# Gate and up projections by seven half-width products in place of eight, with the weight sums on GpSimd

## The chip, the core and the metric

The kernel runs on one core of a Trainium2 chip. TensorE (PE) multiplies, VectorE (DVE), ScalarE (ACT) and GpSimd (POOL) do the elementwise work, SyncE (SP) issues most of the DMAs. The metric is the device time of one execution in microseconds. Before the change the median of three runs is 1285.59 us (1284.54 to 1286.78).

## The reference

Two layers of a decoder over 512 positions of width 1024. The part that the change touches is the feed-forward block of each layer:

```
h = rmsnorm(x, g_pre_ffn[l])
f = silu(h @ w_gate[l]) * (h @ w_up[l])      # (512, 1024) @ (1024, 2816)
f = f @ w_down[l]                            # (512, 2816) @ (2816, 1024)
x = x + rmsnorm(f, g_post_ffn[l])
```

Ahead of it stands a mixing sub-layer: one input projection, four attention groups of four heads, and an output projection with a norm and a residual addition. All values are float32.

## The kernel before

Every float32 operand of a matmul is kept as a pair of reduced-precision tiles, hi and lo: `hi` is a cast (ScalarE) and `lo` the difference of the value and hi (VectorE or GpSimd). A product is three matmuls, `mm3` (lines 195 to 198): hi by hi, hi by lo, lo by hi, all into one PSUM bank. Activations stay transposed on chip, 128 rows of the width by 512 positions per tile, so a block of 128 columns of a weight matrix is the stationary operand and the positions are the moving one.

`weights` (line 160) loads 128x512 values, casts them (line 168) and makes the differences (line 171 on GpSimd, 173 on VectorE; `pool_share` says which chunk goes to GpSimd, and 0 means none). Five raw buffers (WRAW) and six pairs of split buffers (WSPL) go round.

In `ffn` a weight matrix has KF = 22 blocks of 128 columns. For every block j the gate product takes 8 steps over the width, 24 matmuls of 512 columns into one bank, and the up product the same. Then ScalarE applies Silu to the gate bank (line 836) and VectorE multiplies it by the up bank (line 837) into `f`. The down projection follows, with all eight banks as accumulators.

The stage begins while the mixing sub-layer ends. The four row blocks of 128 positions are closed one after the other (`close`, line 738: residual addition, two norms, lines 744 to 749), transposed on TensorE (line 222) and split into `h` (`norm_turn`, line 230). To bridge the wait for the last two of them, the first two blocks of gate and up are computed in halves of 256 positions: first the left halves of all four, then the right halves. The transposes of row blocks 2 and 3 (`turns`) are issued after the second and the fourth left half.

The program is written in one thread; a scheduler puts each engine's instructions in an order and sets the waits between engines. Each engine then works through its own list in that order, so an instruction that waits holds up all behind it on its engine. Tiles with the same tag share a fixed number of buffers, and a new tile waits for the last reader of the old one.

Of the kernel before, what the change touches and what calls it, by code (L numbers as in the profile page):

```python
# [9 lines left out]
F32 = mybir.dt.float32  # L10
# [6 lines left out]
P = 128  # L17
# [59 lines left out]
def f32(ap):  # L77
    return ap.bitcast(F32)
# [3 lines left out]
def decoder(ctx, tc, x, positions, w_in, b_forget, g_mla_q, w_mla_q_up, g_mla_kv, w_mla_kv_up,  # L82
# [190 lines left out]
    def mixing(l, h_in, in_slots, out_slots, w_first):  # L273
# [464 lines left out]
        def close(t, ys):  # L738
# [12 lines left out]
            def turn(behind):  # L751
                with tc.issue_after(behind.ins):
                    norm_turn(t, norm_transpose(hn), h2)
# [3 lines left out]
        turns = []  # L757
# [39 lines left out]
        return xt, h2, turns[2:]  # L797

    def ffn(l, xt, h, turns, f_slots, after):
        fq = []  # L800
# [4 lines left out]
        def w_of(src, j, into=(None, None)):  # L805
            cs = slice(j * P, (j + 1) * P)
            return [weights(src[l, 4 * i * P:4 * (i + 1) * P, cs].rearrange("(k p) c -> p k c", p=P), [4, P], into=into[i])
                    for i in range(2)]

        def block(ps, w, hs):  # L810
            for k in range(KD):
                hi, lo = w[k // 4]
                mm3(ps[:, hs], hi[:, k % 4, :], lo[:, k % 4, :], h[0][k // 4][:, k % 4, hs], h[1][k // 4][:, k % 4, hs],
                    k == 0, k == KD - 1)

        pool_share[0] = SHARE_FFN
        room = keep.tile([P, 6, 512], F32R, name="w_half", tag="slotE")
        room = [room[:, i, :].rearrange("p (k c) -> p k c", c=P) for i in range(4)]
        halves = [(bank(ps_mm, "ps_g"), w_of(w_gate, 0)), (bank(ps_mm, "ps_u"), w_of(w_up, 0)),
                  (bank(ps_mm, "ps_g"), w_of(w_gate, 1)), (bank(ps_o, "ps_u"), w_of(w_up, 1, (room[0:2], room[2:4])))]  # L820
        for hs in (slice(0, 256), slice(256, 512)):
            for i, (ps, w) in enumerate(halves):
                block(ps, w, hs)
                if i % 2 == 1 and turns:
                    turns.pop(0)(last_mm[0])
# [114 lines left out]
```

## Time and profile before

| | |
|---|---|
| runs | 1284.54, 1285.59, 1286.78 us |
| profiled execution | 1284.56 us, span 1282.6 us |
| mean granted TensorE clock | 0.998 |
| busy: PE, DVE, ACT, POOL | 97%, 51%, 46%, 16% |
| gate/up stage, first layer | 279.69 to 524.51 us |
| gate/up stage, second layer | 912.16 to 1156.46 us |

A start time of a row counts from the start of the span. The records of neighbouring instructions of one engine overlap a little, so two in a row take less than the sum of their records; the step from start to start is the time that counts for a stream. "128x512" is partitions by elements. A row with x2 stands for two instructions in a row, with their time together. Where a row names an idle time in brackets, the releaser behind it is what ended it.

### The profile page before, as it was taken

Reading aid. Unit: us, or ns where it says so; the run is one execution under the profiler, and the core shown is the slowest. Engines: PE = TensorE matmul, PEld = TensorE weight load, DVE = VectorE, ACT = ScalarE, POOL = GpSimd, SP = SyncE. Lnnn points to the kernel's source line nnn. Section 1 sums busy time; section 2 is a strip of 40 time slices with the busy share of each in tenths; the row PEclk is TensorE's granted clock in tenths of the full one; section 3 lists DMA queues with packets and bytes.
Section 4 is the critical chain, followed back from the end, with each engine's and each line's share of the span. In section 5 each row is a group of like instructions: output and inputs, shape, how many; then the busy total and the mean of one; then the engine's idle time right before and its main releaser. Section 6 shows DMA issues by size and latency. Waiting matters only on the chain.

```text
span 1282.6 us, 17740 instructions
## 1 busy us (share of the span) xinstructions
PE 1242.6 (97%) x6314; PEld 1041.9 (81%) x6314; DVE 657.0 (51%) x1307; ACT 591.0 (46%) x1287; POOL 201.2 (16%) x287
## 2 busy tenths in 40 slices
PE   6999999999999999999999999999999999999998
PEld 6878877789888888888787788778888888888886
DVE  5876866774333233333466668677742233333334
ACT  6676756754222223333456767666532222233332
POOL 3213334430000000000131324433300000000001
PEclk9999999999999999999999999999999999999999
DMA  7321242522333333333342222334233333332332
GB/s 231 83 59 42 63 117 55 170 75 84 98 99 99 96 94 98 97 94 97 123 125 71 59 56 69 99 91 132 83 107 97 95 96 99 99 98 89 95 97 75
DMA packets 158329, 122.01 MB, mean 95 GB/s; under 512 B 9120, under 2 KB 133152, under 8 KB 158240
## 3 DMA queue, kind: packets, MB, share of 16 engines
q1 hardware_dynamic: 152192, 112.07, 29.8%
q10 hardware_dynamic: 6048, 8.80, 2.6%
q8 instruction: 50, 0.82, 0.3%
q14 instruction: 39, 0.32, 0.1%
HBM read 112.45 MB, written 4.19 MB: 91 GB/s over the span
## 4 chain that ended last, share of the span: by engine, by line
PE 73%; DVE 3%; ACT 3%; DMA 2%; issue 2%; POOL 2%; ACTq 0%; DVEq 0%; POOLq 0%; SPq 0%
PE ps_g L197 6%; PE ps_g L196 6%; PE ps_u L197 6%; PE ps_u L198 6%; PE ps_u L196 6%; PE ps_g L198 6%; PE ps_d L196 6%; PE ps_d L198 6%; PE ps_d L197 6%; PE ps_s L453 2%; PE ps_out L198 2%; PE ps_out L197 2%; PE ps_out L196 2%; PE pT L473 2%; PE ps_qk L196 1%
## 5 line engine op out<-in xcount | busy, mean ns | idle before, releaser
L168 ACT CAST whi<-wraw 128x512 fp32r<-128x512 f32 x348 | 214.2, 621 | 478.4 <-PE ps_g L197 167.4
L173 DVE TENSOR_TENSOR wlo<-wraw,whi 128x512 fp32r<-128x512 f32 (+1 forms) x329 | 239.0, 731 | 368.1 <-ACT whi L168 367.7
L197 PE MATMUL ps_g<-h,whi 128*128 128x512 f32 (+1 forms) x384 | 144.0, 375 | 2.9 <-DVE h L230 2.9
L196 PE MATMUL ps_g<-h,whi 128*128 128x512 f32 (+1 forms) x384 | 143.9, 375 | 1.0 <-ACT h L230 0.8
L198 PE MATMUL ps_g<-h,wlo 128*128 128x512 f32 (+1 forms) x384 | 143.4, 373 | 0.0
L198 PE MATMUL ps_u<-h,wlo 128*128 128x512 f32 (+1 forms) x352 | 133.7, 380 | 0.0
L196 PE MATMUL ps_u<-h,whi 128*128 128x512 f32 (+1 forms) x352 | 133.7, 380 | 0.0
L197 PE MATMUL ps_u<-h,whi 128*128 128x512 f32 (+1 forms) x352 | 133.7, 380 | 0.0
L239 POOL TENSOR_SCALAR rstd<-ssp 128x1 f32<-128x1 f32 x16 | 7.0, 438 | 708.2 <-ACT jk L235 708.1
L198 PE MATMUL ps_d<-whi,fl 128*128 128x512 f32 x288 | 112.2, 389 | 0.0
L196 PE MATMUL ps_d<-whi,fh 128*128 128x512 f32 x288 | 112.1, 389 | 0.0
L197 PE MATMUL ps_d<-wlo,fh 128*128 128x512 f32 x288 | 112.1, 389 | 0.0
L464 POOL TENSOR_SCALAR pr<-pr,den 128x128 f32<-128x128 f32 (+3 forms) x128 | 77.8, 624 | 192.7 <-DVE den L461 189.2
L197 PEld LDWEIGHTS ps_g<-h,whi 128*128 128x128 f32 x384 | 73.0, 190 | 16.5 <-DVE h L230 4.2
L196 PEld LDWEIGHTS ps_g<-h,whi 128*128 128x128 f32 x384 | 73.0, 190 | 14.8 <-ACT h L230 2.3
L198 PEld LDWEIGHTS ps_g<-h,wlo 128*128 128x128 f32 x384 | 73.0, 190 | 12.4
L196 PE MATMUL ps_qk<-h,whi 128*128 128x512 f32 x192 | 76.8, 400 | 0.0
L196 PEld LDWEIGHTS ps_u<-h,whi 128*128 128x128 f32 x352 | 66.2, 188 | 12.5
L198 PEld LDWEIGHTS ps_u<-h,wlo 128*128 128x128 f32 x352 | 66.3, 188 | 12.4
L197 PEld LDWEIGHTS ps_u<-h,whi 128*128 128x128 f32 x352 | 66.2, 188 | 12.4
L198 PE MATMUL ps_qk<-h,wlo 128*128 128x512 f32 x192 | 75.8, 395 | 0.0
L197 PE MATMUL ps_qk<-h,whi 128*128 128x512 f32 x192 | 75.8, 395 | 0.0
(272 smaller groups left out, 2557.7 us busy)
## 6 DMA issues: line engine op xcount, KB each, us to landing
wraw<-in_w_gate_dram SPq DMA_DIRECT2D x88, 256.0 KB, 2.9
wraw<-in_w_up_dram SPq DMA_DIRECT2D x88, 256.0 KB, 2.9
wraw<-in_w_down_dram SPq DMA_DIRECT2D x88, 256.0 KB, 2.8
wraw<-in_w_in_dram SPq DMA_DIRECT2D x72, 256.0 KB, 3.1
wraw<-in_w_out_dram SPq DMA_DIRECT2D x32, 256.0 KB, 3.0
xt<-in_x_dram SPq DMA_DIRECT2D x16, 256.0 KB, 4.6
rope_b<-rope_a ACTq DMA_DIRECT2D x64, 64.0 KB, 2.0
wraw<-in_w_in_dram SPq DMA_DIRECT2D x16, 178.0 KB, 3.4
```

Of the source, the lines that this page charges most:

```text
L168: nc.scalar.copy(hi, raw)
L173: nc.vector.tensor_tensor(lo, raw, f32(hi), op=ALU.subtract)
L196: nc.tensor.matmul(ps, a_hi, b_hi, start=start, stop=False)
L197: nc.tensor.matmul(ps, a_hi, b_lo, start=False, stop=False)
L198: last_mm[0] = nc.tensor.matmul(ps, a_lo, b_hi, start=False, stop=stop)
L239: nc.gpsimd.tensor_scalar(r, ss[:, 0:1], ss[:, 1:2], EPS, op0=ALU.add, op1=ALU.add)
L453: nc.tensor.matmul(ps[:, 0:w], a if a.shape[-1] == P else a[:, qt * P:(qt + 1) * P], b[:, 0:w], start=i == 0, stop=i == n - 1)
L464: nc.gpsimd.tensor_scalar(p, p, den[:, qt - qa:qt - qa + 1], 1.0, op0=ALU.mult, op1=ALU.mult)
L473: nc.tensor.transpose(pt[:, i * P:(i + 1) * P], pr[:, offs[qt] + kt * P:offs[qt] + (kt + 1) * P], ident)
```

## The change

The weight block of two neighbouring j (1024 by 256) is seen as four blocks of 512 by 128, a11, a21 (first half of the width, for j and j+1) and a12, a22 (second half). The activations are four blocks as well: two halves of the width by two halves of the positions. A class `Unit` computes both j with seven products of 512 by 128 by 256 in place of eight (a form of Strassen's method): two with a11 and a12 as they are, one with a22, and four with sums of weight blocks (`combine`, on GpSimd). On the other side four sums of activation blocks (T1 to T4) are made once per layer when row blocks 2 and 3 are turned (class `Operands`), and stored as hi/lo pairs. The results are put together by additions on VectorE, five with an operand in PSUM and two in SBUF per unit, and two copies on ScalarE. The lo part of a22 is made on GpSimd, and so is every second multiplication of gate by up; the other runs on VectorE with both inputs in SBUF.

Of the first three units the two plain products (`first`) are issued ahead of everything else; the transposes of row block 2 are issued after the first unit's, those of row block 3 after the second's. There are no gate/up matmuls of 512 columns any more.

```diff
-        for j in range(KF):
-            if j < 2:
-                (pg, _), (pu, _) = halves[2 * j:2 * j + 2]
-            else:
-                wg, pg = w_of(w_gate, j), bank(ps_mm, "ps_g")
-                block(pg, wg, slice(0, 512))
-                wu, pu = w_of(w_up, j), bank(ps_mm, "ps_u")
-                block(pu, wu, slice(0, 512))
-            f = fq[j]
-            nc.scalar.activation(f, pg, AF.Silu)
-            nc.vector.tensor_tensor(f, f, pu, op=ALU.mult)
...
+        def split_w(raw, pool=False):
+            hi = wp.tile([P, 4, P], F32R, name="whi", tag="whi", bufs=WSPL)
+            lo = wp.tile([P, 4, P], F32R, name="wlo", tag="wlo", bufs=WSPL)
+            nc.scalar.copy(hi, raw)
+            (nc.gpsimd if pool else nc.vector).tensor_tensor(lo, raw, f32(hi), op=ALU.subtract)
+            return hi, lo
+
+        def combine(a, b, op):
+            s = T(F32, "wsum").rearrange("p (k c) -> p k c", c=P)
+            nc.gpsimd.tensor_tensor(s, a, b, op=op)
+            return s
...
+            def result(self, pool, w, b):
+                ps = bank(pool, "ps_7")[:, 0:256]
+                for k in range(4):
+                    mm3(ps, w[0][:, k, :], w[1][:, k, :], b[0][:, k, :], b[1][:, k, :], k == 0, k == 3)
+                return ps
...
+            def one(self, w):
+                nc.scalar.copy(self.dest[0][:, half[1]], self.result(ps_mm, w, ops["11"]))
+
+            def add(self, d, h, ps, to=None):
+                d = self.dest[d]
+                nc.vector.tensor_tensor(d[:, half[h if to is None else to]], ps, d[:, half[h]], op=ALU.add)
+
+            def two(self, w):
+                self.add(0, 1, self.result(ps_o, w, ops["21"]), 0)
+
+            def rest(self, begun):
+                src, j, (d1, d2) = self.src, self.j, self.dest
+                a11 = raw_of(src, j, 0)
+                a21, a22 = raw_of(src, j + 1, 0), raw_of(src, j + 1, 1)
+                s1 = combine(a21, a22, ALU.add)
+                if not begun:
+                    self.one(split_w(a11))
+                s2 = combine(s1, a11, ALU.subtract)
+                w5 = split_w(s1)
+                a12 = raw_of(src, j, 1)
+                s3 = combine(a11, a21, ALU.subtract)
+                w6 = split_w(s2)
+                nc.scalar.copy(d2[:, half[1]], self.result(ps_s, w5, ops["T1"]))
+                s4 = combine(a12, s2, ALU.subtract)
+                w7 = split_w(s3)
+                if not begun:
+                    self.two(split_w(a12))
+                w3 = split_w(s4)
+                self.add(0, 1, self.result(ps_mm, w6, ops["T2"]))
+                ps = self.result(ps_mm, w7, ops["T3"])
+                nc.vector.tensor_tensor(d2[:, half[0]], ps, d1[:, half[1]], op=ALU.add)
+                w4 = split_w(a22, pool=True)
+                self.add(0, 1, d2[:, half[1]])
+                self.add(1, 1, d2[:, half[0]])
+                self.add(0, 1, self.result(ps_s, w3, ops["22"]))
+                self.add(1, 0, self.result(ps_mm, w4, ops["T4"]))
...
+            for d, f, eng in zip(made[i].dest, fq[units[i][1]:units[i][1] + 2], (nc.gpsimd, nc.vector)):
+                if i % 2 == 0:
+                    nc.scalar.activation(f, f, AF.Silu)
+                else:
+                    eng.tensor_tensor(f, f, d, op=ALU.mult)
...
+            for j, b in enumerate((b11, b21)):
+                hi, lo = [f32(self.h[i][j][:, :, ts]) for i in range(2)]
+                nc.gpsimd.tensor_tensor(b, hi, lo, op=ALU.add)
+            p12, p22 = [view(q) for q in pts]
+
+            def split(name, v, low=nc.vector):
+                hi, lo = [q[:, :, ts] for q in self.sums[name]]
+                nc.scalar.copy(hi, v)
+                low.tensor_tensor(lo, v, f32(hi), op=ALU.subtract)
+
+            t1, t3, t4 = [view(T(F32, "hs")) for _ in range(3)]
+            nc.scalar.copy(t4, p12)
+            nc.vector.tensor_tensor(t3, p22, t4, op=ALU.subtract)
+            nc.vector.tensor_tensor(t1, t4, b11, op=ALU.subtract)
+            nc.gpsimd.tensor_tensor(b11, t3, b11, op=ALU.add)
+            split("T1", t1)
+            split("T3", t3)
+            split("22", p22)
+            nc.vector.tensor_tensor(t4, b21, b11, op=ALU.subtract)
+            split("T2", b11, nc.gpsimd)
+            split("T4", t4)
```

How the order of the lists changes is seen at three places.

VectorE in the middle of the stage, before: the splits of one gate and one up block (`wraw` a loaded chunk, `whi` its cast, `wlo` the difference) and the multiplication of the block before (`ps_u` a bank).

```order
L837 TENSOR_TENSOR f_3213<-f_3213,ps_u_3692 128x512
L173 TENSOR_TENSOR wlo_3803<-wraw_3801,whi_3802 128x512
L173 TENSOR_TENSOR wlo_3834<-wraw_3832,whi_3833 128x512
L173 TENSOR_TENSOR wlo_3840<-wraw_3838,whi_3839 128x512
L173 TENSOR_TENSOR wlo_3873<-wraw_3871,whi_3872 128x512
L837 TENSOR_TENSOR f_3213<-f_3213,ps_u_3768 128x512
```

VectorE, the same place after: one gate unit (`f_3213` holds the results of both j), in which the splits of the next unit stand between the additions of this one (`wsum` a sum of weights, `ps_7` a bank, line 849 an addition, 874 the addition into the second result).

```order
L816 TENSOR_TENSOR wlo_4043<-wraw_4034,whi_4042 128x512
L849 TENSOR_TENSOR f_3213<-ps_7_3950,f_3213 128x256
L816 TENSOR_TENSOR wlo_4063<-wsum_4040,whi_4062 128x512
L849 TENSOR_TENSOR f_3213<-ps_7_3968,f_3213 128x256
L816 TENSOR_TENSOR wlo_4071<-wsum_4060,whi_4070 128x512
L874 TENSOR_TENSOR f_3213<-ps_7_3982,f_3213 128x256
L849 TENSOR_TENSOR f_3213<-f_3213 128x256
L816 TENSOR_TENSOR wlo_4091<-wsum_4068,whi_4090 128x512
L849 TENSOR_TENSOR f_3213<-f_3213 128x256
L849 TENSOR_TENSOR f_3213<-ps_7_4002,f_3213 128x256
L816 TENSOR_TENSOR wlo_4095<-wraw_4066,whi_4094 128x512
L849 TENSOR_TENSOR f_3213<-ps_7_4016,f_3213 128x256
```

Where one unit had four splits and one multiplication, there now stand six splits (the sixth, of a sum, stands just ahead of the first row), two additions within SBUF (`f_3213<-f_3213`) and five out of a bank.

GpSimd where the stage begins, before: the last splits of early weights, then the two small instructions (lines 239 and 240) per norm.

```order
L529 TENSOR_TENSOR mix<-mixf,mix 128x256
L171 TENSOR_TENSOR wlo<-wraw,whi 128x512 x3
L171 TENSOR_TENSOR w_half<-wraw,w_half 128x512
L239 TENSOR_SCALAR rstd<-ssp 128x1
L240 TENSOR_TENSOR rstd<-rstd,mhalf 128x1
L239 TENSOR_SCALAR rstd<-ss 128x1
L240 TENSOR_TENSOR rstd<-rstd,mhalf 128x1
```

GpSimd, the same place after (`hback` and `hsum` are sums and splits of activations, `wsum` sums of weights).

```order
L983 TENSOR_TENSOR hback<-h 128x512
L239 TENSOR_SCALAR rstd<-ssp 128x1
L240 TENSOR_TENSOR rstd<-rstd,mhalf 128x1
L983 TENSOR_TENSOR hback<-h 128x512
L239 TENSOR_SCALAR rstd<-ss 128x1
L240 TENSOR_TENSOR rstd<-rstd,mhalf 128x1
L983 TENSOR_TENSOR hback<-h 128x512 x2
L995 TENSOR_TENSOR hback<-hs,hback 128x512
L989 TENSOR_TENSOR hsum_3271<-hback,hsum_3270 128x4x128
L995 TENSOR_TENSOR hback<-hs,hback 128x512
L821 TENSOR_TENSOR wsum<-wraw 128x512
```

The early splits are no longer there, and sums of activations stand between the small instructions of the last norm.

VectorE behind the last normalised row block (`hn`, line 214), before.

```order
L214 SCALAR_TENSOR_TENSOR hn_3203<-xt_2888,rstd_3207,gain_2872 128x512
L214 SCALAR_TENSOR_TENSOR hn_3204<-xt_2889,rstd_3207,gain_2873 128x512
L230 TENSOR_TENSOR h_2894<-hnT_3315,h_2892 128x4x128
L230 TENSOR_TENSOR h_2895<-hnT_3320,h_2893 128x4x128
L230 TENSOR_TENSOR h_2894<-hnT_3377,h_2892 128x4x128
L230 TENSOR_TENSOR h_2895<-hnT_3382,h_2893 128x4x128
L173 TENSOR_TENSOR wlo_3493<-wraw_3491,whi_3492 128x512
L173 TENSOR_TENSOR wlo_3499<-wraw_3497,whi_3498 128x512
L837 TENSOR_TENSOR f_3212<-f_3212,ps_u_3232 128x512
L173 TENSOR_TENSOR wlo_3530<-wraw_3528,whi_3529 128x512
```

VectorE, the same place after, up to the first split of a sum of weights; ahead of the first row shown stand four more of the same kind (lines 993, 994, 849 and 989).

```order
L989 TENSOR_TENSOR h_2895<-hnT_3263,h_2893 128x4x128
L989 TENSOR_TENSOR hsum1_3268<-hs_3276,hsum1_3268 128x4x128
L999 TENSOR_TENSOR hs_3278<-hback_3273,hback_3272 128x512
L993 TENSOR_TENSOR hs_3351<-hnT_3341,hs_3352 128x512
L994 TENSOR_TENSOR hs_3350<-hs_3352,hback_3346 128x512
L989 TENSOR_TENSOR h_2894<-hs_3278,h_2892 128x4x128
L999 TENSOR_TENSOR hs_3352<-hback_3347,hback_3346 128x512
L989 TENSOR_TENSOR hsum1_3268<-hs_3350,hsum1_3268 128x4x128
L989 TENSOR_TENSOR hsum_3269<-hs_3351,hsum_3269 128x4x128
L989 TENSOR_TENSOR h_2895<-hnT_3341,h_2893 128x4x128
L989 TENSOR_TENSOR h_2894<-hs_3352,h_2892 128x4x128
L816 TENSOR_TENSOR wlo_3419<-wsum_3414,whi_3418 128x512
```

Before, the two splits of each of the last two row blocks stood there and then the splits of weights; now it is the differences, sums and splits of four combinations for both row blocks.

## Rows read from the trace of the kernel before

**Rows 1.** The page's busy time of each engine, share of the span, count.
```profile
PE 1242.6 (97%) x6314; PEld 1041.9 (81%) x6314; DVE 657.0 (51%) x1307; ACT 591.0 (46%) x1287; POOL 201.2 (16%) x287
```
**Rows 2.** Table of stretches: us, then each engine's busy us (x count), clock, DMA.
```profile
280.00:284.00 4.00, 4.00 (x21) 3.71 (x20) 3.36 (x6) 2.06 (x6) 0.86 (x2) 0.57 0.42 125
440.00:480.00 40.00, 40.00 (x178) 33.16 (x177) 12.19 (x18) 11.33 (x19) 0.00 (x0) 1.00 0.35 99
```
**Rows 3.** TensorE in order of time: start us, us, instruction; both ends of both stages.
```profile
279.69 0.39 PE L197 MATMUL ps_g<-h,whi 128*128 128x256 f32 x1 [1.02 <-DVE h L230]
...
524.51 0.39 PE L196 MATMUL ps_d<-whi,fh 128*128 128x512 f32 x1
...
912.16 0.39 PE L197 MATMUL ps_g<-h,whi 128*128 128x256 f32 x1 [1.04 <-DVE h L230]
...
1156.46 0.39 PE L196 MATMUL ps_d<-whi,fh 128*128 128x512 f32 x1
```
**Rows 4.** TensorE in order of time: a run of 256 columns, one of 512.
```profile
288.24 0.28 PE L198 MATMUL ps_g<-h,wlo 128*128 128x256 f32 x1
...
293.63 0.28 PE L198 MATMUL ps_u<-h,w_half 128*128 128x256 f32 x1
...
517.71 0.39 PE L196 MATMUL ps_g<-h,whi 128*128 128x512 f32 x1
...
523.83 0.39 PE L196 MATMUL ps_u<-h,whi 128*128 128x512 f32 x1
```
**Rows 5.** Groups by shape: busy us, mean ns of one, idle before and its releaser.
```profile
L173 DVE TENSOR_TENSOR wlo<-wraw,whi 128x512 fp32r<-128x512 f32 x327 | 237.4, 731 | 368.1 <-ACT whi L168 367.7
...
L168 ACT CAST whi<-wraw 128x512 fp32r<-128x512 f32 x346 | 213.3, 622 | 478.4 <-PE ps_g L197 167.4 <-PE ps_u L197 138.3 <-PE ps_d L198 121.0
...
L171 POOL TENSOR_TENSOR wlo<-wraw,whi 128x512 fp32r<-128x512 f32 x19 | 26.5, 1397 | 23.6 <-ACT whi L168 23.5
...
L836 ACT ACTIVATE f<-ps_g 128x512 f32<-128x512 f32 x44 | 26.0, 592 | 0.0
...
L308 DVE TENSOR_TENSOR v<-ps_v,v 128x256 fp32r<-128x256 f32 x24 | 10.0, 418 | 5.6 <-ACT v L307 5.6
```
**Rows 6.** VectorE and GpSimd in order of time, near 135 and 177 us.
```profile
135.17 1.29 POOL L331 TENSOR_TENSOR rope_b<-rope_b,sinT 128x512 f32<-128x512 f32 x1
...
135.18 1.83 DVE L173 TENSOR_TENSOR wlo<-wraw,whi 128x512 fp32r<-128x512 f32 x1
...
176.57 1.81 POOL L331 TENSOR_TENSOR rope_b<-rope_b,sinT 128x512 f32<-128x512 f32 x1 [7.49 <-DMA rope_b<-rope_a]
...
176.53 0.69 DVE L330 TENSOR_TENSOR rope_a<-rope_a,cosT 128x512 f32<-128x512 f32 x1 [1.82 <-DMA rope_b<-rope_a]
177.14 1.79 DVE L173 TENSOR_TENSOR wlo<-wraw,whi 128x512 fp32r<-128x512 f32 x1
```
**Rows 7.** VectorE and GpSimd in order of time, from 268 us.
```profile
268.46 3.22 POOL L171 TENSOR_TENSOR wlo<-wraw,whi 128x512 fp32r<-128x512 f32 x2 [0.84 <-ACT whi L168]
...
268.76 4.08 DVE L173 TENSOR_TENSOR wlo<-wraw,whi 128x512 fp32r<-128x512 f32 x3
```
**Rows 8.** VectorE reading PSUM beside GpSimd, in order of time.
```profile
118.20 1.28 POOL L529 TENSOR_TENSOR mix<-mixf,mix 128x512 fp32r<-128x512 f32 x1 [2.61 <-ACT mix L528]
...
118.64 0.69 DVE L610 TENSOR_TENSOR sp_lo<-natT,sp_hi 96x512 fp32r<-96x512 f32 x1 [0.45 <-ACT sp_hi L609]
```
**Rows 9.** VectorE in order of time, two splits in a row.
```profile
855.67 1.29 DVE L173 TENSOR_TENSOR wlate<-wraw,wlate 128x512 fp32r<-128x512 f32 x2 [1.79 <-ACT wlate L168]
```
**Rows 10.** The last normalised row block and its transposes, in order of time.
```profile
291.11 1.42 DVE L214 SCALAR_TENSOR_TENSOR hn<-xt,rstd,gain 128x512 f32<-128x512 f32 x2 [1.89 <-POOL rstd L240]
...
293.75 1.04 PE L222 MATMUL hnT<-cst,hn 128*128 128x128 f32 x8
```

More of the change, by code (lines that the diff above doesn't have):

```diff
@@ L803, in ffn @@
             fq += [q[:, i, :] for i in range(4)]
[L805 to L825, printed above, removed]
@@ new lines, in ffn, with __init__, first @@
+        half = slice(0, 256), slice(256, 512)
+        class Unit:
+            def __init__(self, src, j, dest):
+                self.src, self.j, self.dest = src, j, dest
+            def result(self, pool, w, b):
[3 more added lines that the diff above has]
+                return ps
+            def first(self):
+                src, j = self.src, self.j
+                self.one(split_w(raw_of(src, j, 0)))
+                self.two(split_w(raw_of(src, j, 1)))
+            def one(self, w):
[31 more added lines that the diff above has]
+                self.add(1, 0, self.result(ps_mm, w4, ops["T4"]))
@@ new lines, in ffn, with make, close_unit @@
+        pool_share[0] = 0
+        ops = {}
+        units = []
+        for j in range(0, KF, 2):
+            units.append((w_gate, j))
+            units.append((w_up, j))
+        def make(i):
+            src, j = units[i]
+            dest = (fq[j], fq[j + 1]) if i % 2 == 0 else (H("u1"), H("u2"))
+            return Unit(src, j, dest)
+        def close_unit(i):
+            for d, f, eng in zip(made[i].dest, fq[units[i][1]:units[i][1] + 2], (nc.gpsimd, nc.vector)):
[3 more added lines that the diff above has]
+                    eng.tensor_tensor(f, f, d, op=ALU.mult)
@@ L839, in ffn @@
+        made = {}
+        ops["11"], ops["21"] = turns.blocks()
+        early_units = 3
+        for i in range(early_units):
+            made[i] = make(i)
+            made[i].first()
+            if i < 2:
+                turns.later(i + 2, last_mm[0])
+        ops.update(turns.combined())
+        for i in range(len(units)):
+            if i not in made:
+                made[i] = make(i)
+            made[i].rest(i < early_units)
+            close_unit(i)
         tail = 4
@@ L874, in ffn, with __init__, blocks, turn @@
             after(t)
+    class Operands(list):
+        def __init__(self, h):
+            super().__init__()
+            self.h = h
+            self.sums = {}
+        def blocks(self):
+            h = self.h
+            return [tuple(h[i][j][:, :, 0:256] for i in range(2)) for j in range(2)]
+        def turn(self, t, pts):
+            if t < 2:
+                norm_turn(t, pts, self.h)
+                return
+            if t == 2:
+                m = slot("M2", F32R, "hsum1")
+                two = lambda q: q.rearrange("p (k t) -> p k t", k=4)
+                e = keep.tile([P, 6, 512], F32R, name="hsum", tag="slotE")
+                self.sums["T1"] = [m[:, 2 * i:2 * i + 2, :].rearrange("p a (b t) -> p (a b) t", b=2) for i in range(2)]
+                self.sums["T3"] = [e[:, 2 * i:2 * i + 2, :].rearrange("p a (b t) -> p (a b) t", b=2) for i in range(2)]
+                self.sums["T2"] = [two(keep.tile([P, PRW], F32R, name="hsum2", tag="pr", bufs=2)[:, 0:1024]) for i in range(2)]
+                self.sums["T4"] = [self.h[i][0][:, :, 256:512] for i in range(2)]
+                self.sums["22"] = [self.h[i][1][:, :, 256:512] for i in range(2)]
+            ts = slice((t - 2) * P, (t - 1) * P)
+            view = lambda q: q.rearrange("p (k t) -> p k t", k=4)
+            b11, b21 = [view(R(F32, "hback")) for _ in range(2)]
+            for j, b in enumerate((b11, b21)):
[17 more added lines that the diff above has]
+            split("T4", t4)
+        def later(self, t, behind):
+            self[t](behind)
+        def combined(self):
+            return self.sums
```

10 lines of the change are left out of this document (7 added, 3 removed).

## The prediction

> **What bounds the kernel now.** I read the page's busy line first, then a table of stretches, then the order of time on TensorE, and last VectorE and GpSimd side by side. The busy line has TensorE at 97% and no other engine above 51% [rows 1]. In the middle of the first gate/up stage TensorE is busy for all of 40 us at the full clock, VectorE for 12.2, ScalarE for 11.3 and GpSimd for nothing [rows 2]. So the stage that changes is bound by the number of matmuls and their pitch, and the helpers have two thirds of it free. It runs from 279.69 to 524.51 us in the first layer and from 912.16 to 1156.46 in the second [rows 3]: 244.8 and 244.3 us, 244.6 on average.
>
> The pitch of a matmul comes from two places in TensorE's order [rows 4]. Between 288.24 and 293.63 lie 45 steps of 256 columns, 0.1198 us each. Between 517.71 and 523.83 lie 27 steps of 512 columns, 0.2267 each. A half-width matmul costs 53% of a full one, not 50%.
>
> **The change, part by part: TensorE.** Call two neighbouring blocks of 128 columns of one of the two weight matrices a unit; there are 22 per layer. Before, a unit is 48 matmuls of 512 columns, 10.9 us. After, it is 7 products of 12 matmuls of 256 columns, 84 x 0.1198 = 10.06. Two of the 22 units ran at half width before, with 96 x 0.1198 = 11.5. Per layer that is 20 x 10.88 + 2 x 11.5 = 240.6 before and 22 x 10.06 = 221.4 after: TensorE alone would save 19 us per layer, 38 in all. An eighth of 240.6 would be 30; the pitch at half width takes 11 of it.
>
> **VectorE and GpSimd, the steady units.** Before, a unit asks VectorE for 4 splits and one multiplication, and GpSimd for nothing. After, the order rows in the section on the change show for VectorE: 6 splits (128x512), 2 additions of 256 columns and in every second unit a multiplication, all with two inputs in SBUF; and 5 additions of 256 columns with one input in PSUM. GpSimd gets 4 sums, one split and in every second unit a multiplication. By themselves these fit. A split has a record of 0.69 us, but two in a row take 1.29 together [rows 9], so I take 0.61 each; an addition of 256 columns out of PSUM has a record near 0.42 [rows 5], less the same overlap 0.34, and I take that for the two in SBUF as well. VectorE: 6 x 0.61 + 2 x 0.34 + 0.31 + 5 x 0.34 = 6.35 us. GpSimd: the trace shows no sum, but the subtraction and the multiplication of the same shape take 1.29 undisturbed [rows 6]; 5.5 x 1.29 = 7.1. ScalarE: 7 casts at 0.62, two copies and on average one activation at no more than 0.59 each [rows 5], 6.1. All stand below 10.06.
>
> They don't fit together. At 135.17 GpSimd starts a multiplication, at 135.18 VectorE a split, and the split's record is 1.83 instead of 0.69: it ends 0.55 after GpSimd's end [rows 6]. At 176.57 it is the other way round: GpSimd's record grows to 1.81 and ends 1.16 after VectorE's, and the next split again waits, 1.79. From 268.46 on, two GpSimd splits and three VectorE splits alternate strictly: 4.08 us for three splits, which is 2 x 1.71 + 0.69 [rows 7]. So an instruction of GpSimd with two inputs and one of VectorE with two SBUF inputs exclude each other, and a pair costs 1.16 + 0.55 = 1.71. A VectorE instruction that reads PSUM is not touched: at 118.64 one takes 0.69 in the middle of a GpSimd instruction [rows 8].
>
> This bounds a unit. If every GpSimd instruction holds VectorE up for 1.71 - 0.61 = 1.10, a unit takes 6.35 + 5.5 x 1.10 = 12.4 us. If all five PSUM additions run beside GpSimd, 1.7 of that goes. A floor comes from the two-input instructions alone, packed without a gap: 5.5 x 1.16 + 6.5 x 0.55 + 2 x 0.28 = 10.5. In VectorE's order 5 of the 8.5 two-input instructions are followed by a PSUM addition, so I let 5/8.5 of the 5.5 GpSimd instructions hide one of 0.34: 1.1 us, and a unit of 11.3. That is 1.2 above TensorE's new need and 0.4 above the old one: the bound moves from TensorE to the pair, and TensorE waits for splits.
>
> The first three units have two of their products done ahead of the rest. What is left of each is 4 splits, 2 additions, 4 PSUM additions and the same 5.5 on GpSimd. By the same steps that is 10.8 with nothing hidden, 9.4 packed, and I take 9.7.
>
> The Trainium skill has a rule that speaks against this change. GPSIMD Engine Reference, section "3. Performance versus the Vector engine", puts a two-input elementwise operation at about twice VectorE's time and says to leave such work to VectorE. Here the ratio of the records is 1.29 to 0.69, 1.9, so the trace agrees. With the four sums on VectorE, 4 x 0.61 would replace 4 x 1.10: a unit of 6.35 + 2.44 + 1.5 x 1.10, less 0.3 for PSUM additions beside GpSimd: 10.1, about what TensorE needs. As the change has it, the sum is 11.3.
>
> **The start of the stage.** In the old order the fourth row block of activations is normalised at 291.11 to 292.53, its transposes run at 293.75 [rows 10], and 256-column products of the first four weight blocks keep TensorE supplied. In the new order six products (6 x 12 x 0.1198 = 8.6 us) stand ahead of the sums of activations. The order rows show what VectorE does between the last normalised row and the first split of a summed weight, that split included: 16 instructions, 11 with two SBUF inputs. 15 x 0.61 + 0.34 = 9.5 us. GpSimd has 8 two-input instructions in the same stretch, 8 x 1.10 = 8.8, of which the five PSUM instructions can hide 2.8. So 15.5 to 18.3, in the middle 16.9. Two of GpSimd's sums (hback) stand ahead of the small rstd instructions of the fourth block and can push it by 0 to 2 us; I take 1. The first product of a sum then starts at 292.5 + 1 + 16.9 = 310.4, 30.7 us into the stage (28.3 to 33.1), in which TensorE has 8.6 us of products and two groups of transposes. It stands still for some 19 us. After the much shorter pause of the old start its granted clock averaged 0.57 from 280 to 284 [rows 2], the lower level of 1.2 GHz for most of it; after this one it will fall again, but then TensorE isn't the bound, and I add nothing.
>
> **The end of the stage.** The down projection needs all banks, so it waits for the last two PSUM additions; splits of its weights are in the queue by then. 0 to 3 us, I take 1.
>
> **The sum.** Per layer 30.7 + 3 x 9.7 + 19 x 11.3 + 1 = 275.5 against 244.6: +30.9, for two layers +62. The profiled run took 1284.56 us, 2.0 above its span and 1.0 below the median of the runs: 1284.6 + 62 = 1346.6, as a median 1347. The low ends (28.3, 9.4, 10.5, 0) give 256.0, +23, 1307. The high ends (33.1, 10.8, 12.4, 3) give 304.1, +119, 1404.
>
> The other stages keep their order but for a few neighbours that change places; I cost that at nothing, since TensorE leads there as before and the instructions are the same.
>
> **Rivals.** *TensorE stays the bound.* GpSimd's instructions would fall where VectorE waits for a product anyway. For it: VectorE's own 6.35 leaves 3.7 us of a 10.06 us unit. Against it: GpSimd needs the shared path for 5.5 x 1.16 = 6.4, and 3.7 + 1.7 of PSUM additions are only 5.4. With no hold at all, the start takes 292.5 + 9.5 - 279.7 = 22.3, and the stage 22.3 + 3 x 7.2 + 19 x 10.06 = 235.0, -9.6 per layer: 1266, faster. It decides at a mean of 10.3 us per steady unit; with the start at 30.7 the point is 9.9, below what TensorE itself needs.
>
> *Only the start costs.* 30.7 + 21.6 + 191.1 = 243.4 per layer, -2.4 in all: 1283, at the edge of no change.
>
> *The ring of split buffers closes.* A unit makes seven split pairs and there are six buffers (WSPL), so ScalarE's cast of the next unit waits for a product of this one, and behind it in ScalarE's queue stand the copies that free banks. If one chain of cast and held split (0.62 + 1.79 = 2.4 us) is exposed per unit, steady units take 13.7: +46 per layer on the forecast, 1438. Against it: between the product that frees the tightest buffer (the sixth in TensorE's order) and the one that needs it lie three products, 4.3 us.
>
> **How the numbers follow.** The pair sets the pace: 0.80, all of it slower. The ring closes: 0.09, slower. TensorE stays the bound: 0.07. Only the start costs: 0.04, half of it faster. About 0.2% (2.6 us) is what a measurement of this kernel tells from no change. Faster 0.09, same 0.02, slower 0.89. The range 1305 to 1405 is the span of the forecast's ends; what lies outside is the rivals' 0.2.
>
> **What the new profile would show.** Right: in the steady stretch VectorE's splits with a mean well above 0.69 (near 1.2 to 1.4) and records of 1.8 beside GpSimd's, TensorE idle about a tenth, 11.3 us from unit to unit; a pause on TensorE of 15 us or more near 295 to 310 in the first layer; 256-column matmuls at 0.12. Wrong: splits at 0.69 and units of 10.1; ScalarE waiting on TensorE for a buffer with VectorE idle (the ring); or a start under 24 us.

## The result, and the profile after

The changed kernel takes **1483.51 us** (median of 4 runs, 1481.85 to 1485.83), the kernel before in the same comparison 1285.34. The ratio is 1.154, 95% interval 1.153 to 1.156. The prediction had the side right, 1347 us and a range that ended at 1405: of the added time, 198 us, it saw 62.

First the page's busy line of the changed kernel, as in [rows 1], and three stretches of its table of stretches (us, then each engine's busy us and count, TensorE's granted clock, DMA share, GB/s).

```profile
PE 1275.4 (86%) x7706; PEld 1137.9 (77%) x7706; DVE 947.9 (64%) x1709; ACT 708.2 (48%) x1523; POOL 572.2 (39%) x537
```

```profile
290.00:300.00 10.00, 4.52 (x19) 3.89 (x19) 8.67 (x12) 4.09 (x8) 6.47 (x5) 0.50 0.05 15
300.00:310.00 10.00, 4.41 (x15) 3.56 (x16) 8.70 (x9) 4.06 (x8) 8.61 (x6) 0.50 0.08 15
440.00:480.00 40.00, 29.79 (x220) 29.18 (x220) 22.84 (x36) 14.06 (x26) 19.48 (x14) 0.91 0.28 79
```

In the steady stretch of [rows 2], 440 to 480 us, TensorE went from 40.0 busy to 29.8. But VectorE is busy for only 22.8 and GpSimd for 19.5. The forecast wanted a pair of engines that blocks itself without a gap; here all engines have gaps, and that points to a loop of waits. In order of time, for [rows 10], the last normalised rows and TensorE's first product of a sum (start us, us, instruction, idle time ahead of it and what ended it); then, for [rows 3], the group of the first down-projection matmuls (min, median and max in ns, first and last start):

```profile
289.54 1.41 DVE L214 SCALAR_TENSOR_TENSOR hn<-xt,rstd,gain 128x512 f32<-128x512 f32 x2 [1.51 <-POOL rstd L240]
...
304.13 0.58 PE L196 MATMUL ps<-hsum,whi 128*128 128x256 f32 x1 [6.69 <-ACT whi L815]
```

```profile
L196 PE MATMUL ps_d<-whi,fh x288: 389/389/396, 622.5 to 1453.1; 128*128 128x512 f32 x144
```

The first layer's stage ends at 622.5, not at 524.5: 342.8 us from the old start at 279.69, where 275.5 was forecast and 244.8 stood before. To measure a unit I take the one addition on VectorE that each unit makes of product T3; over 16 units from the sixth on its mean distance is **15.13 us**, against 11.3 forecast. The first product of a sum stands at 304.1, 24.4 us after the old start, against 30.7. The last 19 units, forecast at 11.3, have a mean of 14.81: 66.7 us per layer too much. Beside them the start is 6.3 too short, the first three units 5.3 too long (34.4 us from the first product of a sum to the third of these additions, against 3 x 9.7) and the end 1.6 too long, in sum the 67.3 us between 342.8 and 275.5. Twice that is 134.6 of the miss of 136 (the second layer's stage is some 3 us longer still): it is the steady unit.

What the unit waits for is in the table of waits of the first stage (320 to 620 us): engine, line, what it waited for: us in total, times, longest.

```profile
POOL wsum L821 <- DMA wraw<-in_w_gate_dram: 50.5, 13, 5.5
POOL wsum L821 <- DMA wraw<-in_w_up_dram: 42.6, 11, 5.7
POOL wsum L821 <- DVE wlo L816: 14.4, 5, 4.0
...
PE ps L198 <- POOL wlo L816: 68.1, 19, 5.8
...
SPq L809 <- POOL wsum L821: 107.6, 22, 5.8
SPq L809 <- POOL wlo L816: 89.6, 19, 5.3
```

GpSimd's sums wait 24 times, 3.9 us each, for weights from DRAM; TensorE waits 19 times, 3.6 us each, for a low split on GpSimd; and the queue that issues the loads (SPq) waits for GpSimd, 22 times for a sum and 19 times for that split. So GpSimd waits for loads that wait for GpSimd. GpSimd over one and a half units, with two rows of the load queue set between (the second is the last of the three loads of the first), then TensorE:

```profile
442.07 1.27 POOL L821 TENSOR_TENSOR wsum<-wraw,wsum 128x512 f32<-128x512 f32 x1 [3.31 <-DMA wraw<-in_w_gate_dram]
443.31 1.70 POOL L816 TENSOR_TENSOR wlo<-wraw,whi 128x512 fp32r<-128x512 f32 x1
...
445.04 8.73 SPq L809 DMA_DIRECT2D wraw<-in_w_up_dram  x3
...
453.40 0.37 SPq L809 DMA_DIRECT2D wraw<-in_w_up_dram  x1
...
449.00 1.29 POOL L821 TENSOR_TENSOR wsum<-wraw 128x512 f32<-128x512 f32 x1 [3.99 <-DVE wlo L816]
450.37 1.30 POOL L821 TENSOR_TENSOR wsum<-wsum,wraw 128x512 f32<-128x512 f32 x1
451.63 1.75 POOL L821 TENSOR_TENSOR wsum<-wraw 128x512 f32<-128x512 f32 x1
453.33 1.75 POOL L898 TENSOR_TENSOR f<-f,u 128x512 f32<-128x512 f32 x1
456.66 1.48 POOL L821 TENSOR_TENSOR wsum<-wraw,wsum 128x512 f32<-128x512 f32 x1 [1.58 <-PE ps L198]
458.11 1.44 POOL L816 TENSOR_TENSOR wlo<-wraw,whi 128x512 fp32r<-128x512 f32 x1
463.60 1.30 POOL L821 TENSOR_TENSOR wsum<-wraw 128x512 f32<-128x512 f32 x1 [4.05 <-DMA wraw<-in_w_gate_dram]
```

```profile
445.06 0.39 PE L198 MATMUL ps<-h,wlo 128*128 128x256 f32 x1 [4.47 <-POOL wlo L816]
445.29 0.28 PE L196 MATMUL ps<-h,whi 128*128 128x256 f32 x1
...
445.87 0.42 PE L197 MATMUL ps<-h,whi 128*128 128x256 f32 x1
...
448.64 0.41 PE L198 MATMUL ps<-h,wlo 128*128 128x256 f32 x1
...
449.06 0.28 PE L197 MATMUL ps<-h,whi 128*128 128x256 f32 x1
...
450.97 0.28 PE L198 MATMUL ps<-h,wlo 128*128 128x256 f32 x1
...
459.60 0.58 PE L198 MATMUL ps<-h,wlo 128*128 128x256 f32 x1 [2.71 <-POOL wlo L816]
```

Read it so. The split of a22 (L816) stands behind all four sums of the *next* unit. It frees a raw buffer: it ends at 445.01, the next loads of a21 and a22 are issued from 445.04 on, and the following sum (a21 + a22) starts at 449.00; a unit later it ends at 459.55 and that sum starts at 463.60, each time after some 4 us of nothing. (At 449.00 a VectorE split that ended last is named; 24 of these waits name the load.) Two sums later s3 is the last reader of a11 and a21: it ends at 453.38, the load of a12 is issued at 453.40, and s4 waits for that load (3.31 in the unit before, at 442.07). TensorE's last product of a unit needs the split's result and stands still for 4.47 and 2.71 us.

### The profile page after: what moved, and what is told of

It is laid out like the page before. It is cut to its first block, busy times and chain, and to the rows that moved or that the text cites. A ratio compares the mean times of both kernels' runs of the same rounds, so it can differ in the third digit from the quotient of the medians.

```text
span 1482.0 us, 21831 instructions
## 1 busy us (share of the span) xinstructions
PE 1275.4 (86%) x7706; PEld 1137.9 (77%) x7706; DVE 947.9 (64%) x1709; ACT 708.2 (48%) x1523; POOL 572.2 (39%) x537
## 5 line engine op out<-in xcount | busy, mean ns | idle before, releaser
L198 PE MATMUL ps<-h,wlo 128*128 128x256 f32 x704 | 228.1, 324 | 135.6 <-POOL wlo L816 135.6
L198 PEld LDWEIGHTS ps<-h,wlo 128*128 128x128 f32 x704 | 159.1, 226 | 143.3 <-POOL wlo L816 143.3
L196 PE MATMUL ps<-h,whi 128*128 128x256 f32 x704 | 222.1, 315 | 6.6 <-DVE u L849 4.0
L197 PE MATMUL ps<-h,whi 128*128 128x256 f32 x704 | 221.1, 314 | 0.1
L173 DVE TENSOR_TENSOR wlo<-wraw,whi 128x512 fp32r<-128x512 f32 (+1 forms) x164 | 121.0, 745 | 132.5 <-ACT whi L168 132.0
L821 POOL TENSOR_TENSOR wsum<-wraw 128x512 f32<-128x512 f32 x88 | 132.7, 1508 | 164.6 <-DMA wraw<-in_w_up_dram 79.9
L816 DVE TENSOR_TENSOR wlo<-wsum,whi 128x512 fp32r<-128x512 f32 x176 | 177.5, 1009 | 26.4 <-ACT whi L815 22.8
L196 PE MATMUL ps<-hsum,whi 128*128 128x256 f32 x528 | 153.0, 290 | 15.4 <-ACT whi L815 15.4
L196 PEld LDWEIGHTS ps<-h,whi 128*128 128x128 f32 x704 | 159.1, 226 | 7.8 <-DVE u L849 3.9
L197 PEld LDWEIGHTS ps<-h,whi 128*128 128x128 f32 x704 | 158.4, 225 | 0.6 <-DVE h L230 0.5
L816 DVE TENSOR_TENSOR wlo<-wraw,whi 128x512 fp32r<-128x512 f32 x88 | 91.2, 1043 | 98.1 <-ACT whi L815 98.0
L198 PE MATMUL ps<-hsum,wlo 128*128 128x256 f32 x528 | 152.5, 290 | 1.5 <-DVE wlo L816 1.5
L197 PE MATMUL ps<-hsum,whi 128*128 128x256 f32 x528 | 152.2, 288 | 0.9 <-POOL hsum L989 0.9
L815 ACT CAST whi<-wraw 128x512 fp32r<-128x512 f32 x132 | 81.6, 619 | 114.0 <-PE ps L197 54.9
```

The source lines that it names most:

```text
L173: nc.vector.tensor_tensor(lo, raw, f32(hi), op=ALU.subtract)
L196: nc.tensor.matmul(ps, a_hi, b_hi, start=start, stop=False)
L197: nc.tensor.matmul(ps, a_hi, b_lo, start=False, stop=False)
L198: last_mm[0] = nc.tensor.matmul(ps, a_lo, b_hi, start=False, stop=stop)
L815: nc.scalar.copy(hi, raw)
L816: (nc.gpsimd if pool else nc.vector).tensor_tensor(lo, raw, f32(hi), op=ALU.subtract)
```

## The experiments

Theory A: five raw buffers and GpSimd's order close a ring of loads; under it lies the shared path of VectorE and GpSimd at the price that was forecast. Rival B: the shared path alone costs 15 us per unit. Rival C: the ring of six split buffers. "Unit" is the mean distance of T3 additions in the first layer (16 units from the sixth); "stage ends" is the first matmul of the down projection there. The kernel before took 1283.3 to 1284.0 beside them.

| kernel | us | ratio to before, 95% | unit | stage ends |
|---|---|---|---|---|
| changed kernel | 1483.5 | 1.153 to 1.156 | 15.13 | 622.5 |
| e1 fixed a21, a22 | 1348.7 | 1.050 to 1.053 | 11.30 | 554.7 |
| e2 a22 in own buffers | 1385.8 | 1.078 to 1.082 | 12.23 | 575.9 |
| e3 split of a22 on VectorE | 1348.6 | 1.049 to 1.052 | 11.29 | 555.0 |
| e4 both | 1346.0 | 1.047 to 1.051 | 11.38 | 553.3 |
| e12 own split pair | 1485.1 | 1.155 to 1.159 | 14.95 | 625.4 |
| e13 split of a22 earlier | 1374.0 | 1.069 to 1.072 | 12.07 | 567.0 |
| e5 sums on VectorE | 1346.5 | 1.047 to 1.051 | 11.54 | 552.3 |
| e10 e5, a22 in own buffers | 1327.1 | 1.031 to 1.035 | 11.09 | 544.1 |
| e9 all on VectorE | 1287.4 | 1.002 to 1.004 | 10.15 | 524.3 |
| e6 e9, a22 in own buffers | 1283.2 | 0.999 to 1.001 | 10.07 | 522.7 |
| e11 e6, no activation sums | 1252.5 | 0.974 to 0.977 | 10.07 | 507.3 |
| e7 e6, six units early | 1276.7 | 0.993 to 0.996 | - | 519.3 |
| e8 six gate units early | 1276.5 | 0.993 to 0.996 | - | 519.1 |

### The ring: e1 to e4

e1 takes half of a unit's loads away.

```
-                a21, a22 = raw_of(src, j + 1, 0), raw_of(src, j + 1, 1)
+                a21, a22 = fixed     # two buffers, loaded once per layer
```

> What it leaves out: the two blocks a21 and a22 are loaded once per layer into two buffers of their own and used by all 22 units, so the result is not that of the reference; casts, splits, sums and products are the same in number and order. It takes away half of a unit's loads, and with five buffers for the two that are left no load is late. Theory A (GpSimd's order closes a ring of raw buffers: its last instruction of a unit frees a buffer, the load of the next block takes 3.4 to 4.0 us, the next unit's first sum waits for it, and s4 waits in the same way for a load that s3 released): GpSimd's two waits of 4.0 and up to 3.3 us per unit go, a steady unit falls from 15.0 us to the 11.3 to 12 that the shared path allows, about 1483.5 - 40 x 3.35 = 1350 us (1335 to 1370). Rival B (the shared path of VectorE and GpSimd alone costs that much, the loads only fill its gaps): unit stays near 15, 1475 to 1490. Rival C (the six split buffers close the ring): 1475 to 1490 as well.

Measured 1348.7, unit 11.30: 1.3 us from what theory A said, B and C out. What is left looks as the forecast drew it (a table of stretches; VectorE's groups by shape from 400 to 500 us, count | busy us, mean ns | idle us; GpSimd and VectorE in order of time):

```profile
440.00:480.00 40.00, 36.25 (x296) 35.44 (x294) 38.39 (x49) 16.85 (x32) 29.52 (x20) 1.00 0.16 48
```

```profile
L817 DVE TENSOR_TENSOR wlo<-wsum,whi 128x512 fp32r<-128x512 f32 x36 | 41.5, 1154 | 0.0
```

```profile
450.22 1.75 POOL L817 TENSOR_TENSOR wlo<-f,whi 128x512 fp32r<-128x512 f32 x1
451.93 1.74 POOL L822 TENSOR_TENSOR wsum<-f 128x512 f32<-128x512 f32 x1
...
449.35 1.45 DVE L817 TENSOR_TENSOR wlo<-wsum,whi 128x512 fp32r<-128x512 f32 x1
451.06 1.45 DVE L817 TENSOR_TENSOR wlo<-wsum,whi 128x512 fp32r<-128x512 f32 x1
```

VectorE is now busy for 38.4 of 40, its splits of sums have a mean of 1.15 us where [rows 5] has 0.73, and where both engines have a two-input instruction ready they alternate, one pair every 1.71 us (450.22 to 451.93, 449.35 to 451.06).

e2 gives a22 two buffers of its own (two blocks of f that no unit uses), e3 moves its split to VectorE, e4 does both.

```
-                a21, a22 = raw_of(src, j + 1, 0), raw_of(src, j + 1, 1)
+                a21, a22 = raw_of(src, j + 1, 0), raw_of(src, j + 1, 1, spare[(src is w_up) * 1])   # e2, e4
-                w4 = split_w(a22, pool=True)
+                w4 = split_w(a22)                                                                    # e3, e4
```

> a22 is loaded into two buffers of its own in place of the ring of five, the other three blocks keep the ring. GpSimd's instructions and order stay. Theory A: only half of the ring opens. s4's load no longer hangs on s3 of the same unit (3.3 us, part of it covered every second unit by the multiplication), but a22's buffer is freed by the low split that stands right ahead of the next unit's first sum, so the wait of 4.0 us stays: a unit of 12 to 13.5 us, 1365 to 1425 us. Rivals B (shared path) and C (split buffers): 1475 to 1490.

> The split of a22 goes from GpSimd to VectorE, where it stands ahead of the next unit's splits; nothing else. Theory A: the last product of a unit no longer waits for an instruction that stands behind the next unit's sums, and a21's buffer is freed by VectorE in time; s4's wait for the load that s3 released stays. A unit of 11.5 to 12.7 us, 1345 to 1390 us. Rival B (shared path alone): one GpSimd instruction less at 1.10 against one VectorE split more at 0.61, a unit shorter by 0.5, 1463. Rival C: the split buffers are used as before, 1475 to 1490.

> Both edits: a22 in two buffers of its own, and its split on VectorE. Theory A: both waits of GpSimd for a load go. What is left is the shared path: VectorE 6.96, 4.5 GpSimd instructions x 1.10, less 1.1 hidden = 10.8 us per unit, 1483.5 - 40 x 4.2 = 1315 us (1295 to 1345). Rival B: 1463. Rival C: 1475 to 1490.

1385.8, 1348.6 and 1346.0: the first two as theory A had them (e3's unit, 11.29, a little under its 11.5); one opens half of the ring, the other all that matters. In e3 GpSimd's sums still wait 25 times for loads from 320 to 554 us, 54 us in all, but VectorE is busy for 39.8 of the 40 us from 440. In e4 I expected the saved GpSimd instruction to show as 0.5 us per unit (1315) and it did not: 11.38. Once the ring is open, moving one instruction from GpSimd to VectorE changes little (1348.7 in e1, 1346.0 in e4).

### The other ring, and the place in the order: e12, e13

```
+            if pool:
+                hi, lo = ops["pair"]      # e12: the split pair of a22 in the free third of slotE
...
+                w4 = split_w(a22, pool=True)     # e13: ahead of s4
                 s4 = combine(a12, s2, ALU.subtract)
...
-                w4 = split_w(a22, pool=True)
```

> Against the changed kernel one edit: the split pair of a22 (high and low) lies in the free third of the tile of activation sums, so the ring of six split pairs serves six pairs per unit in place of seven. Engines and raw buffers stay. Theory A (ring of raw buffers through GpSimd's order): no change, 1470 to 1490. Rival C (ring of split buffers; ScalarE waits 226 us in all for TensorE's last read of a pair in the changed kernel's trace): a unit shorter by 1 us or more, 1440 or less.

> One line of the changed kernel stands higher in the code: the split of a22 is written ahead of s4 in place of behind the products T2 and T3. In GpSimd's order it then stands behind the next unit's first two sums in place of behind all four; engines, buffers and instruction counts stay, and the next loads of a21 and a22 no longer hang on it together with s3 and s4. Theory A, sharpened (the place in GpSimd's order of the instruction that frees a22's buffer, not the engine it runs on): GpSimd's wait ahead of a unit's first sum goes or shrinks below 2 us, the last product no longer waits 2.7 us for it, a unit of 11.5 to 13 us, 1350 to 1405 us. Rival (it had to leave GpSimd, because a split there holds VectorE and delays the order whatever its place): 1460 to 1490.

e12 is 1485.1: the 226 us in which ScalarE waits for split buffers are a wait of an engine that has time, and rival C is out, though the trace bears the sign that the prediction gave for that ring (ScalarE waiting for TensorE, VectorE idle). e13 is 1374.0: one line moved, same engines and buffers, and 109 of the 135 us that e1 gives back are back. GpSimd in e13, in order of time:

```profile
448.84 1.28 POOL L821 TENSOR_TENSOR wsum<-wraw 128x512 f32<-128x512 f32 x1 [1.28 <-DMA wraw<-in_w_up_dram]
450.20 1.61 POOL L821 TENSOR_TENSOR wsum<-wsum,wraw 128x512 f32<-128x512 f32 x1
451.77 1.74 POOL L816 TENSOR_TENSOR wlo<-wraw,whi 128x512 fp32r<-128x512 f32 x1
453.48 1.74 POOL L898 TENSOR_TENSOR f<-f,u 128x512 f32<-128x512 f32 x1
455.18 1.48 POOL L821 TENSOR_TENSOR wsum<-wraw 128x512 f32<-128x512 f32 x1
...
461.75 1.30 POOL L821 TENSOR_TENSOR wsum<-wraw 128x512 f32<-128x512 f32 x1 [3.65 <-DVE wlo L816]
```

The split (L816) stands between the second and the third sum, so its buffer is loaded while GpSimd has other work. So the place in the order closes the ring. It does not open altogether: the wait ahead of a unit's first sum, expected below 2 us, is 1.28 in this unit and 3.65 in the next (last row), for loads that were issued from 456.68 on, as the third sum ended. The other 25 us are this rest and the engine that the split runs on (1374.0 against e3's 1348.6), not separated.

### The shared path: e5, e6, e9, e10

```
-            nc.gpsimd.tensor_tensor(s, a, b, op=op)
+            nc.vector.tensor_tensor(s, a, b, op=op)         # e5, e6, e9, e10: sums of weights
-                w4 = split_w(a22, pool=True)
+                w4 = split_w(a22)                           # e6, e9
-(nc.gpsimd, nc.vector)):
+(nc.vector, nc.vector)):                                    # e6, e9: the multiplication
```

> One word against the changed kernel: the four sums of weights of a unit go from GpSimd to VectorE; GpSimd keeps the low split of a22 and every second unit's multiplication, the ring of five raw buffers stays. Theory A (raw loads released by GpSimd's order, and under it the price of the shared path): both go. The split of a22 no longer stands behind sums, VectorE needs 6.35 + 4 x 0.61 + 1.5 x 1.10 - 0.3 = 10.1 us per unit beside TensorE's 10.06, a unit of 10.1 to 10.8: from e4's 1346.0 at 11.3 per unit, 44 units x 0.9 less, 1306 us (1293 to 1322). Rival (VectorE was 92 to 97% busy from 400 to 520 us in e1, e3 and e4, so 2.4 us of work more only moves the bound): unit of 11.3 or longer, 1346 to 1375.

> Sums, the split of a22 and all multiplications on VectorE, a22 in two buffers of its own: GpSimd has nothing in a steady unit. VectorE: 11 of 128x512 with two SBUF inputs x 0.61, half a multiplication x 2 = 0.61, 2 x 0.34 and 5 x 0.34 = 9.7 us, under TensorE's 10.06. Theory A: a unit of 10.1 to 10.4, TensorE bound, 1346.0 - 44 x 1.1 = 1298 us (1286 to 1310); what is left above the kernel before is the start of the stage (24.4 us to the first product of a sum, then some 2 us at the lower clock). Rival as for e5: VectorE stays the bound, 1346 or more.

> e6 without the two buffers for a22: everything on VectorE, all four blocks in the ring of five. e5 missed (1346.5 where 1306 was expected) and differs from e6 (1283.2) in three things: the ring, the split of a22 and half the multiplications on GpSimd. If the ring of five raw buffers is what cost e5 (in its trace VectorE's sums wait 1.1 to 1.4 us for a load, twice in two units), it closes here too, through VectorE's order: a unit near 11, 1310 to 1347. If GpSimd's remaining instructions cost it: as e6, 1278 to 1290.

> The other half of that question: e5 with a22 in two buffers of its own, GpSimd keeps the split of a22 and half the multiplications. If the ring cost e5: VectorE 6.35 + 2.44 + 1.65 - 0.3 = 10.1 us beside TensorE's 10.06, 1283 to 1300. If GpSimd's instructions (pairs on the shared path, a last product that waits for a GpSimd split) cost it: 1325 to 1347.

e5 missed, 1346.5 where 1306 was expected. The number is the low end of its rival, but the rival's reason doesn't hold: VectorE is busy for 35.6 of the 40 us from 440. e6 came out 3 us below its range. e9 came out as the second of its two cases: with everything on VectorE the ring of five costs 4 us in all, not 30 to 60. So did e10: 1327.1 against e6's 1283.2 shows that the 1.5 instructions per unit left on GpSimd cost 44 us. The other 19 us of e5 are the ring of five raw buffers, which costs that much as long as GpSimd has the split of a22. Three rows of e10's VectorE, one of its groups from 400 to 500 us and a row of its GpSimd:

```profile
450.02 1.53 DVE L817 TENSOR_TENSOR wlo<-wraw,whi 128x512 fp32r<-128x512 f32 x1 [0.18 <-ACT whi L816]
454.15 0.69 DVE L822 TENSOR_TENSOR wsum<-wraw,f 128x512 f32<-128x512 f32 x1 [1.68 <-DMA f<-in_w_up_dram]
460.54 1.78 DVE L900 TENSOR_TENSOR f<-f,u 128x512 f32<-128x512 f32 x1
...
L822 DVE TENSOR_TENSOR wsum<-wraw,f 128x512 f32<-128x512 f32 x9 | 6.2, 693 | 8.7 <-DMA f<-in_w_up_dram 8.5
...
449.60 1.40 POOL L817 TENSOR_TENSOR wlo<-f,whi 128x512 fp32r<-128x512 f32 x1 [10.11 <-ACT whi L816]
```

GpSimd's split starts late here too, after 10.11 us of waiting for its cast, and what it frees is late for VectorE's next sum (1.68), while the pairs hold VectorE (1.53 and 1.78). These sums wait 8.7 us in nine units, 0.97 per unit, and e10's unit is 1.02 longer than e6's; but the held splits cost VectorE time as well and the work that GpSimd took off it gives time back, so how much is the load and how much the hold was not separated. In e6 TensorE stands still for nothing from 440 to 480 us, and VectorE's splits are back at one length (table of stretches; group from 400 to 500 us):

```profile
300.00:310.00 10.00, 2.79 (x11) 2.52 (x12) 8.80 (x13) 5.03 (x9) 3.37 (x2) 0.50 0.22 72
...
440.00:480.00 40.00, 40.00 (x336) 40.00 (x335) 39.41 (x77) 21.27 (x40) 0.00 (x0) 1.00 0.40 116
```

```profile
L817 DVE TENSOR_TENSOR wlo<-wsum,whi 128x512 fp32r<-128x512 f32 x41 | 28.0, 683 | 0.3
```

The loads move 116 GB/s there, where the changed kernel moved 79 in the same stretch: what its sums waited for were loads issued late, not a lack of bandwidth.

### The start, and two versions a little under the kernel before: e11, e7, e8

e11 leaves the sums of activations away, e7 and e8 put more products ahead of them.

```
-        for i in range(early_units):                # 3
+        begun = [0, 1, 2, 4, 6, 8]                  # e7; e8: [0, 2, 4, 6, 8, 10]
+        for n, i in enumerate(begun):
```

> e6 without the sums of activations: the third and fourth row block are only normalised, turned and split as the kernel before does it, and the products T1, T2 and T3 read the first column block of h in place of the sums; what it computes is not the reference. All sums of weights and all 154 products per layer stay. It prices the start: the 16 VectorE and 8 GpSimd instructions between the last normalised row and the first split of a summed weight go. Where the start is 24.4 us and the products and transposes in it some 11, TensorE's pause of 10 to 13 us per layer goes and with it some 2 us at the lower clock: 1283.2 - 2 x 12 = 1259 us (1252 to 1266). If VectorE's total sets the stage whatever the pause: 1275 or more.

> e6 with six units begun ahead of the sums of activations in place of three (gate 0, up 0, then gates 2, 4, 6, 8), so 12 products of TensorE stand there in place of 6. If the pause at the start is what is left: 8.6 us of products fill part of the 10 us in which TensorE stands still from 290 to 304 us, against some 3.6 us more of splits on VectorE ahead of the first summed weight: 3 to 7 us less per layer than e6, 1284 if e6 is 1298 (6 to 14 less than e6). If VectorE's total sets the stage, as e6 within 3 us.

> As e7, but the six units are all of the gate matrix, and the third and fourth row block of activations are turned after two and four of them in place of one and two: more products stand ahead of the sums, and the sums start later. Expected as e7, within 5 us of it; below it if TensorE's pause shrinks further, above it if the later sums push the first summed product.

e11: 1252.5, at the low edge; the sums of activations cost 30.7 us, 15.4 per layer, some 3 more than their pause was priced at. With neither them nor GpSimd in the way the seven products show what they give TensorE: 31 us against the kernel before. e7 and e8 give 6.5 and 6.7 us against e6, as expected, and both end half a per cent below the kernel before: 0.9948 (0.993 to 0.996) and 0.9947, small but clear of 1. From 300 to 310 us TensorE in e7 is busy for 5.22, nearly twice e6's 2.79:

```profile
300.00:310.00 10.00, 5.22 (x24) 5.02 (x25) 9.18 (x15) 3.18 (x7) 3.21 (x2) 0.67 0.42 131
```

## Why the prediction was wrong, point by point

**The step that failed** is the steady unit. It counted GpSimd's instructions ("5.5 GpSimd instructions", each holding VectorE for 1.10) and took them as always ready: "a unit of 11.3". It had a price for running beside VectorE and none for waiting. Measured were 15.13, and 11.30 with half of the loads taken away (e1). Each sum needs one or two raw blocks, there are five buffers for them where a unit loads four blocks, and in GpSimd's queue the last reader of a block stands behind the next unit's sums. GpSimd's order, to be had ahead of any run, shows it:

```
L821 TENSOR_TENSOR wsum_4186<-wraw_4182,wraw_4184 128x512
L821 TENSOR_TENSOR wsum_4206<-wsum_4186,wraw_4180 128x512
L821 TENSOR_TENSOR wsum_4214<-wraw_4180,wraw_4182 128x512
L821 TENSOR_TENSOR wsum_4234<-wraw_4212,wsum_4206 128x512
L816 TENSOR_TENSOR wlo_4145<-wraw_4038,whi_4144 128x512
```

The buffer of `wraw_4038`, a block of the unit before, is given back behind four sums of this one. The bound of 12.4 was a bound of work, so the range ended at 1405.

**The price of the pair** was right where both engines are ready: e1 shows the 1.71 us that were put together from three places in [rows 6, 7]. With half of the loads away (e1) the unit is 11.30 where the sum said 11.3, the stage ends 275.0 us after the old start where it said 275.5, and the kernel takes 1348.7 where the prediction said 1347. That this is so close is in part luck. In e1 the start took 24.6, not 30.7, and the first three units 34.8, not 29.1, and the two errors cancel. And the same steps with fewer instructions on GpSimd gave 10.8 for e4 and 10.1 for e5 and e10, where 11.38, 11.54 and 11.09 were measured: 1.10 us per GpSimd instruction, less a part that hides, is not a price that can be carried from unit to unit.

**TensorE's part** was right: 84 matmuls at 0.1198, 10.06; e6, e9 and e11 have units of 10.07 to 10.15. Over the kernel e11 gives 31 us back, not 38.

**The start** came earlier than its lowest bound, 28.3: the last rows were normalised by 290.95 (292.5 had been taken, plus 1 for GpSimd), and from there to the first product of a sum it took 13.2 us, not 15.5 to 18.3. The clock fell as forecast: from 290 to 310 the granted clock is 0.50, and the first products of sums run at the lower level, 1.2 GHz (0.21 us per matmul). Whether "I add nothing" was wrong for the changed kernel is not shown. 15.2 us lie between the first product of a sum and the first T3 addition (319.3), but there VectorE waits 4.82 us for a cast that waits for the second unit's first sum on GpSimd:

```profile
316.48 1.23 DVE L816 TENSOR_TENSOR wlo<-wsum,whi 128x512 fp32r<-128x512 f32 x1 [4.82 <-ACT whi L815]
...
315.83 0.62 ACT L815 CAST whi<-wsum 128x512 fp32r<-128x512 f32 x1 [4.10 <-POOL wsum L821]
```

e11, whose granted clock stays at 1.00 from 290 to 310, gives back 15.4 us per layer against e6; how much of that is the clock was not separated.

**The rivals.** The ring of split buffers was the right kind of mechanism for the wrong buffers: "six buffers" for seven pairs is tight and costs nothing (e12), five raw buffers for four blocks closes, because it is freed late. The two rivals in which TensorE stays the bound needed GpSimd's work to be free; it isn't, and where it is gone (e6) the time, 1283.2, is that of the kernel before and of the rival in which only the start costs (1283).

**The rule on the two engines.** In e9 the sums stand on VectorE and the unit is 10.15 us. The Trainium skill (GPSIMD Engine Reference, "3. Performance versus the Vector engine") says to leave such two-input work to VectorE; the runs agree, 15.13 against 10.15. The 10.1 that the prediction worked out for the move of the sums alone was wrong: that run, e5, has 11.54 (11.09 with a22 in its own buffers, e10). Only with the split and the multiplications moved too is the unit 10.07 to 10.15, and then TensorE's 10.06 sets it.

**Two slips** in the working changed nothing of the forecast. 2 x 1.71 + 0.69 is 4.11, not the 4.08 of the row. And from the prediction's own terms the steady unit at which the change breaks even is (244.6 - 22.3 - 21.6) / 19 = 10.6 and, with the start at 30.7, 10.1, not 10.3 and 9.9; so the second does not lie below what TensorE needs, 10.06.

## What to carry to other kernels

When a change gives an in-order engine new work, list for each of its instructions which buffer its end frees, who loads into that buffer, and which instruction of the same engine waits for that load. If the freeing instruction stands ahead of the waiting one with nothing in between, the load's whole latency (here 3.4 to 4 us) is in every turn of the loop, however idle all engines look. Count buffers against the time from load to last reader in the order as scheduled, not against the number of blocks, and try the cheapest cure first: moving one line of code, the last reader, further up gave back 109 us here.

## What the runs showed of the hardware

- After a wait of 4.47 us TensorE's first matmuls (from 445.06) ran at the full clock (2.4 GHz, records of 0.28), then the pitch was 0.213 us from 445.87 to 448.64 (13 steps), the lower level of 1.2 GHz, and 0.119 again from 449.06 to 450.97 (16 steps). After the next wait, 2.71 us, the lower level stood from the first matmul on (0.213 from 459.99 to 462.33, 11 steps). So each of these two stalls also cost half of some 3 us of TensorE's pace; the granted clock from 440 to 480 us was 0.91.
- A VectorE that is busy for 39.4 of 40 us and a TensorE that is busy for all of them go together (e6): with GpSimd silent VectorE can be run almost full without a wait on TensorE.
- Two-input instructions of VectorE and GpSimd, both always ready, settle into one pair every 1.71 us (e1), the figure that collisions in the kernel before gave [rows 6, 7].
